# Merge and output projection of a hybrid encoder block: three chain steps per block of products in place of two

## The chip, the core and the metric

One core of one Trainium2 chip runs the whole layer in one launch. The metric is the device time of a run in microseconds (us). Before the change three runs took 2575.63, 2579.93 and 2582.38 us, median 2579.93 us.

## What is computed

The reference is one encoder layer on x, 2048 tokens of width 1024, all in float32. Cut to what matters here:

```python
h = rmsnorm(x, norm1_g); proj = h @ w_in
ya = windowed_gqa(...)            # 8 heads, band of +-128
ym = mlstm_branch(...)            # forward and backward recurrence, 4 heads of 128
gates = sigmoid(mg + merge_b)
u = gates[..., :1024] * (ya @ w_branch_attn) + gates[..., 1024:] * (ym @ w_branch_mlstm)
x = x + u @ w_out
# hier_moe on rmsnorm(x): group logits, expert logits, top 2 of 8 experts of the top group,
# tokens sorted by expert, silu(x @ w_gate) * (x @ w_up) @ w_down, added back by weight
```

The backward recurrence (`flip` in the reference) goes through the tokens from the last to the first. A merge of a token needs `ym` of both directions, and the routing of a token needs its merged x.

## The kernel before, in words

**Stages.** The program has three stages. F takes four chunks of 512 tokens (c = 0 to 3), makes all projections, the attention and the forward recurrence. B (merge and output projection) goes through the chunks backwards, c = 3, 2, 1, 0. M is the mixture of experts, one expert after the other. The change lies in B.

**Products of B.** A chunk has a BR part and a WO part. BR: four pieces of branch weights (`branch_piece`, 256 output columns each), and per piece two column blocks `cb`; a column block is 12 products of `yahi`/`yalo` (attention) and 12 of `ymhi`/`ymlo` (recurrence), 512 wide; so 192 products. `uevac` (L1157 to L1166) then merges the two sums by the gates on VectorE and splits the result into `uhi` (ScalarE, L1165) and `ulo` (VectorE, L1166). WO: four pieces of `w_out`, and per piece four groups `wo_group`, one for each 128 tokens, of 24 products 256 wide; so 16 groups, 384 products. `wevac` (L1173, VectorE) adds each group's sum to the residual tile `x1`. The sums of attention products and of WO groups lie in the PSUM pool `mmp`, two buffers.

**Weights.** `Stream.advance` brings a piece from memory on SP's queue (`wraw`, L220), splits it into a high half on ScalarE (`whi`, L236) and a low half on GpSimd (`wlo`, L239).

**Chains.** Everything else of B is written as generators in named queues of the class `Chains`: `mh` and `ml` (backward recurrence, `mhead` and `mtile`, four tiles of 128 tokens per chunk, one chunk ahead of the merge), `mp` (`mpost`: norm and gate of a tile's output, transposed at L812), `yp` (`yprep`: loads the next chunk's y tiles), and `rt` (`norm2` and `route` of the chunk merged before). `run_mms` writes the products and after each block of them (6 in BR, 12 in WO) lets the weight stream advance by one step and the chains by `tick_n[0]` steps, in turn over the queues:

```python
            if i % nsub == nsub - 1:
                if i == nsub - 1:
                    flush_late()
                ws.advance()
                ch.tick(tick_n[0])
```

`tick_n[0]` is 4 from the end of F until B's loop starts, 2 in B's loop, and 4 again for the last ten WO groups of c = 0. Where the chains are not done in time, `ch.drain` runs them to the end at once: `yp` at the start of BR, `ml` and `mp` ahead of the third WO piece. The order of writing is a priority: when the kernel is built, a scheduler puts each engine's instructions into their final order from it, and moves ready work ahead.

**How y reaches the merge.** `mpost` of a tile that is written after `direct["c"] = c - 1` was set (at a chunk's first WO piece) splits its transposed output straight from PSUM into `ymhi` (L817, ScalarE) and `ymlo` (L818, VectorE). A tile that is written earlier copies it to `hf` (L821, ScalarE) and stores it to `ym_s` in memory (L822, SP's queue); `yprep` loads it back into `yr` (L1136, SP's queue, two buffers) and splits it (L1138 on ScalarE, L1140 on VectorE).

**Routing.** `route` of a chunk computes the slots of its tokens: two counting products (L1298, L1299), then on VectorE the sum of the two choices (L1296 ahead of them), the slot numbers cast to integers (`si`, L1321) and the entries `ent`, one buffer: token numbers copied from the constant `tokid` (L1318) and weights (L1319). `put` (L1331) then writes them with eight indirect DMAs from GpSimd's queue into `slot_s`, each after the one before has landed. The token copies L1318 depend on nothing but `tokid` and the free buffer.

Of the kernel before, what the change touches and what calls it, by code (L numbers as in the profile page):

```python
# [102 lines left out]
def body(tc, A, out, scr_ext=None, upto="all"):  # L103
    nc = tc.nc
    scr_ext = scr_ext or {}
    es = ExitStack()
    with es:
        pass
        _body(tc, nc, A, out, scr_ext, upto, es)


def _body(tc, nc, A, out, scr_ext, upto, es):
# [213 lines left out]
    tick_n = [2]  # L326
# [1087 lines left out]
        held.extend((si, ent, i, 1) for i in range(2))  # L1414
        yield

    tick_n[0] = 2
    first_b = True
    while pi < len(plan):
        c, kind, i = plan[pi]  # L1420
# [440 lines left out]
```

## Time and profile before

| what | value |
|---|---|
| runs | 2575.63, 2579.93, 2582.38 us; median 2579.93 us |
| profiled execution | 2579.44 us, of which 2577.6 us are its span from the first to the last instruction |
| TensorE (PE) | 2420.9 us busy, 94% of the span |
| weight loads (PEld) | 2090.1 us, 81% |
| VectorE (DVE) | 1660.2 us, 64% |
| ScalarE (ACT) | 1312.2 us, 51% |
| GpSimd (POOL) | 931.0 us, 36% |
| mean granted TensorE clock | 0.977 of full speed |

Products are pipelined on TensorE and their ends are modelled, so a busy share near 100% still has slack in it; idle time in front of a product is idle. An engine's idle time before an instruction is given with what ended it. The stage that the change touches runs from about 1193 us to 1712 us of the span.

### The profile page before, as it was taken

Reading aid. Unit: us, or ns where it says so; the run is one execution under the profiler, and the core shown is the slowest. Engines: PE = TensorE matmul, PEld = TensorE weight load, DVE = VectorE, ACT = ScalarE, POOL = GpSimd, SP = SyncE. Lnnn points to the kernel's source line nnn. Section 1 sums busy time; section 2 is a strip of 40 time slices with the busy share of each in tenths; the row PEclk is TensorE's granted clock in tenths of the full one; section 3 lists DMA queues with packets and bytes.
Section 4 is the critical chain, followed back from the end, with each engine's and each line's share of the span. In section 5 each row is a group of like instructions: output and inputs, shape, how many; then the busy total and the mean of one; then the engine's idle time right before and its main releaser. Section 6 shows DMA issues by size and latency. Waiting matters only on the chain. (4 is left out here: it accounts for less than half of the span.)

```text
span 2577.6 us, 39210 instructions
## 1 busy us (share of the span) xinstructions
PE 2420.9 (94%) x13932; PEld 2090.1 (81%) x13933; DVE 1660.2 (64%) x2795; ACT 1312.2 (51%) x2564; POOL 931.0 (36%) x918
## 2 busy tenths in 40 slices
PE   7999999999999999997898889979999999999997
PEld 6889988899889989886787778867777777777776
DVE  4465455664556655578659484677866776778665
ACT  4455455464556555454342333236755665667554
POOL 5543444443543533333444445432221222122111
PEclk9999999999999999998999999989999999999999
DMA  4535434453445445556867565459998897889974
GB/s 146 162 116 169 148 109 125 144 181 94 127 138 158 134 121 163 182 174 193 244 193 209 176 180 168 131 192 322 363 318 294 255 328 235 299 255 361 343 245 103
DMA packets 348413, 515.33 MB, mean 200 GB/s; under 512 B 25019, under 2 KB 212500, under 8 KB 348188
## 3 DMA queue, kind: packets, MB, share of 16 engines
q1 hardware_dynamic: 332140, 460.03, 54.4%
q0 software_dynamic: 14880, 48.20, 8.0%
q10 hardware_dynamic: 1168, 4.21, 0.4%
q8 instruction: 127, 2.08, 0.3%
q14 instruction: 98, 0.80, 0.1%
HBM read 420.83 MB, written 91.54 MB: 199 GB/s over the span
## 5 line engine op out<-in xcount | busy, mean ns | idle before, releaser
L239 POOL TENSOR_TENSOR wlo<-wraw,whi 128x512 fp32r<-128x512 f32 (+1 forms) x422 | 574.1, 1390 | 403.2 <-ACT whi L236 386.4
L1573 DVE TENSOR_TENSOR elo<-raw,ehi 128x1024 fp32r<-128x1024 f32 x256 | 299.4, 1219 | 27.5 <-ACT ehi L1572 27.4
L319 PE MATMUL mm<-hThi,whi 128*128 128x512 f32 x768 | 306.4, 399 | 0.0
L319 PE MATMUL mm<-hTlo,whi 128*128 128x512 f32 x768 | 304.9, 397 | 0.0
L319 PE MATMUL mm<-hThi,wlo 128*128 128x512 f32 x768 | 303.6, 395 | 0.0
L236 ACT ACTIVATE whi<-wraw 128x512 fp32r<-128x512 f32 (+1 forms) x424 | 234.0, 622 | 130.0 <-PE mm L319 75.9
L319 PE MATMUL mm<-whi,hThi 128*128 128x256 f32 (+1 forms) x896 | 262.1, 292 | 3.0 <-ACT ev L908 1.8
L1572 ACT ACTIVATE ehi<-raw 128x1024 fp32r<-128x1024 f32 x256 | 254.1, 1050 | 19.7 <-DMA raw<-w_expert_up 17.8
L319 PE MATMUL mm<-wlo,hThi 128*128 128x256 f32 (+1 forms) x896 | 257.5, 287 | 1.5 <-POOL wlo L239 1.5
L319 PE MATMUL mm<-whi,hTlo 128*128 128x256 f32 (+1 forms) x896 | 258.1, 288 | 0.0
L1687 POOL DMA_INDIRECT out<-y,idx x32 | 55.4, 1731 | 448.8 <-DVE y L1686 223.2
L1619 PE MATMUL mm<-ehi,xhi 128*128 128x512 f32 x512 | 205.5, 401 | 0.0
L1619 PE MATMUL mm<-ehi,xlo 128*128 128x512 f32 x512 | 201.0, 393 | 0.4 <-DVE xlo L1598 0.4
L319 PEld LDWEIGHTS mm<-whi,hThi 128*128 128x128 f32 x896 | 172.3, 192 | 5.4 <-ACT ev L908 2.1
L319 PEld LDWEIGHTS mm<-wlo,hThi 128*128 128x128 f32 x896 | 172.4, 192 | 2.5 <-POOL wlo L239 1.8
L319 PEld LDWEIGHTS mm<-whi,hTlo 128*128 128x128 f32 x896 | 171.9, 192 | 0.9 <-DVE hTlo L449 0.2
L319 PEld LDWEIGHTS mm<-hThi,wlo 128*128 128x128 f32 x768 | 144.4, 188 | 31.1
L319 PEld LDWEIGHTS mm<-hThi,whi 128*128 128x128 f32 x768 | 144.6, 188 | 29.1
L319 PEld LDWEIGHTS mm<-hTlo,whi 128*128 128x128 f32 x768 | 144.5, 188 | 28.3
L1622 PE MATMUL mm<-elo,xhi 128*128 128x512 f32 x512 | 159.0, 392 | 0.0
L1573 DVE TENSOR_TENSOR elo<-rawd,ehi 128x1024 fp32r<-128x1024 f32 x128 | 151.4, 1220 | 11.6 <-ACT ehi L1572 11.4
L833 DVE SCALAR_TENSOR_TENSOR cacc<-cstg,colv,cacc 128x512 f32<-128x512 f32 x128 | 108.1, 845 | 58.4 <-ACT cacc L830 56.5
(456 smaller groups left out, 5932.0 us busy)
## 6 DMA issues: line engine op xcount, KB each, us to landing
wraw<-w_in SPq DMA_DIRECT2D x152, 512.0 KB, 4.3
raw<-w_expert_gate SPq DMA_DIRECT2D x128, 512.0 KB
raw<-w_expert_up SPq DMA_DIRECT2D x128, 512.0 KB, 10.1
rawd<-w_expert_down SPq DMA_DIRECT2D x64, 1024.0 KB, 12.5
mg_s<-evg SPq DMA_DIRECT2D x64, 256.0 KB, 3.8
gt<-mg_s SPq DMA_DIRECT2D x32, 512.0 KB, 6.5
wraw<-w_out SPq DMA_DIRECT2D x32, 512.0 KB, 7.3
mqk<-qk_s SPq DMA_DIRECT2D x16, 512.0 KB, 5.6
```

Of the source, the lines that this page charges most:

```text
L236: nc.scalar.activation(hi[:, ks, :W], r[:, k:k + 2, :W], AF.Copy)
L239: eng.tensor_sub(lo[:, ks, :W], r[:, k:k + 2, :W], hi[:, ks, :W].bitcast(F32))
L319: nc.tensor.matmul(o, l, r, start=st, stop=sp)
L833: nc.vector.scalar_tensor_tensor(acc, stg[:, r:r + CH], colv[:, j, r:r + 1], acc, op0=OP.mult, op1=OP.add)
L1572: nc.scalar.activation(dst[0], src, AF.Copy)
L1573: nc.vector.tensor_tensor(dst[1], src, dst[0].bitcast(F32), op=OP.subtract)
L1619: nc.tensor.matmul(self.gu[h], x_[:, k % 4, :], self.wt(k)[0][:, h, :], start=k == 0 and i == 0, stop=False)
L1622: nc.tensor.matmul(self.gu[h], self.xs[k // 4][0][:, k % 4, :], self.wt(k)[1][:, h, :], start=False, stop=k == KT - 1)
L1687: nc.gpsimd.indirect_dma_start(out=out, out_offset=bass.IndirectOffsetOnAxis(ap=self.idx, axis=0), in_=y, in_offset=None, compute_op=OP.add)
```

## The change

One number: the steps that the chains get after each block of products in B's loop, up to the last ten groups of c = 0.

```diff
@@ -1414,7 +1414,7 @@
         held.extend((si, ent, i, 1) for i in range(2))
         yield
 
-    tick_n[0] = 2
+    tick_n[0] = 3
     first_b = True
     while pi < len(plan):
         c, kind, i = plan[pi]
```

What it moves is seen in the built order alone. Up to the first merged column blocks of c = 3, and from the expert stage on, each engine's order is as it was; between them the number of TensorE rows is the same, and rows change places.

**TensorE, the counting products of the routing of c = 3's tokens.** First before, then with the change (`whi,uhi` are WO products, `yahi` and `ymhi` BR products, `mv`, `mw`, `Cst` the recurrence's, `mw` at L812 its output):

```order
L741 MATMUL m<-Cst,mqk 128x129
L1298 LDWEIGHTS before
L1298 MATMUL Rb<-ohb,before 128x4x32
L1299 LDWEIGHTS onesb
L1299 MATMUL Rb<-ohb,onesb 128x4x32
L319 MATMUL mm<-whi,ulo 128x256
```

```order
L1298 LDWEIGHTS before
L1298 MATMUL Rb<-ohb,before 128x4x32
L1299 LDWEIGHTS onesb
L1299 MATMUL Rb<-ohb,onesb 128x4x32
L741 MATMUL m<-Cst,mqk 128x129
L812 MATMUL m<-ident,mw 128x128 x4
L319 MATMUL mm<-yahi,wlo 128x512
```

They stood behind WO product 29 of c = 2 and stand now behind BR product 179 of it; for the routing of c = 2's tokens, behind WO product 5 of c = 1, now behind BR product 177. The outputs of the recurrence (L812) stood in c = 2 behind BR product 168 and WO products 76, 143 and 206, and stand behind BR product 179 and WO products 92, 191 and 222; in c = 1 the last stood behind WO product 196 and stands behind 224; in c = 3 the four stood behind BR products 96 and 169 and WO products 48 and 111, and stand behind BR products 66 and 133 and WO products 7 and 81.

**VectorE, the token copies in the WO part of c = 2.** Before, then with the change (`x_` are the residual tiles, one row per WO group; `hf`, `og`, `mw`, `Cst` are the recurrence's):

```order
L1173 SCALAR_TENSOR_TENSOR x_14384<-mm,x_14384 128x256
L1173 SCALAR_TENSOR_TENSOR x_14386<-mm,x_14386 128x256
L1318 COPY ent<-tokid 128x4 x2
L1173 SCALAR_TENSOR_TENSOR x_14380<-mm,x_14380 128x256
L1173 SCALAR_TENSOR_TENSOR x_14382<-mm,x_14382 128x256
```

```order
L772 SCALAR_TENSOR_TENSOR Cst<-Cst,mil,m 128x129 x2
L1173 SCALAR_TENSOR_TENSOR x_14515<-mm,x_14515 128x256
L808 TENSOR_TENSOR mw<-mw,og 128x512
L1318 COPY ent<-tokid 128x4 x2
L772 SCALAR_TENSOR_TENSOR Cst<-Cst,mil,m 128x129 x2
L1173 SCALAR_TENSOR_TENSOR x_14509<-mm,x_14509 128x256
```

The copies stood behind the 12th group of c = 2 and stand behind the 8th. The cast of the slot numbers (L1321) stood behind the 4th group and stands behind the 2nd. Between cast and copies lie 30 VectorE instructions before, 8 of them L1173, and 39 with the change, 6 of them L1173. In c = 1 the cast stands behind the 2nd group as before; the copies stood behind the 10th and stand behind the 7th, with 37 instructions between, 5 of them L1173.

**ScalarE, the recurrence's outputs in the WO part of c = 2.** Before, then with the change:

```order
L817 ACTIVATE ymhi<-m 128x4x128
L236 ACTIVATE whi<-wraw 128x2x256 x4
L748 ACTIVATE mdn<-m 128x2 x2
L817 ACTIVATE ymhi<-m 128x4x128
L236 ACTIVATE whi<-wraw 128x2x256 x4
L817 ACTIVATE ymhi<-m 128x4x128
```

```order
L821 ACTIVATE hf<-m 128x512
L236 ACTIVATE whi<-wraw 128x2x256 x4
L1138 ACTIVATE ymhi<-yr 128x4x128
L748 ACTIVATE mdn<-m 128x2 x2
L821 ACTIVATE hf<-m 128x512
L236 ACTIVATE whi<-wraw 128x2x256 x4
```

Before, seven of the twelve tiles went straight into `ymhi` (L817: one in c = 3, three in c = 2, three in c = 1). With the change none does: all twelve are copied (L821), stored and loaded back (L1138).

## Rows read from the trace of the kernel before

**Rows 1.** Busy time by engine, one stretch per part of B (BR, WO of c=3, 2, 1).

```profile
core 0: us, PE busy (x) PEld busy (x) DVE busy (x) ACT busy (x) POOL busy (x), PEclk, DMA share, GB/s
1192.80:1253.60 60.80, 54.58 (x252) 44.72 (x253) 50.71 (x82) 20.60 (x49) 27.98 (x34) 0.93 0.85 254
1253.70:1313.20 59.50, 55.29 (x452) 54.03 (x452) 24.36 (x48) 16.49 (x31) 24.01 (x21) 0.97 0.67 197
1313.20:1378.00 64.80, 62.03 (x333) 52.28 (x333) 54.67 (x102) 27.76 (x70) 29.53 (x29) 0.97 0.70 209
1378.00:1456.70 78.70, 61.52 (x481) 59.43 (x480) 44.16 (x97) 19.46 (x45) 35.02 (x36) 0.91 0.58 169
1456.70:1520.50 63.80, 61.41 (x340) 51.25 (x339) 55.36 (x107) 27.06 (x69) 31.24 (x30) 1.00 0.71 210
1520.50:1590.20 69.70, 58.41 (x472) 57.51 (x471) 38.80 (x86) 20.35 (x45) 35.50 (x33) 0.95 0.49 148
```

**Rows 2.** Timeline of VectorE, WO of c=2 (start us, us; idle before and releaser in brackets).

```profile
1405.07 1.24 DVE L1321 CAST si<-sl 128x8 int32<-128x8 f32 x1
...
1430.26 0.42 DVE L1173 SCALAR_TENSOR_TENSOR x<-mm,x 128x256 f32<-128x256 f32 x1 [2.42 <-PE mm L319]
1443.68 2.63 DVE L1318 COPY ent<-tokid 128x4 f32<-128x4 f32 x2 [12.99 <-DMA slot_s<-ent,si]
```

**Rows 3.** Timeline of TensorE, WO of c=2, around its longest idle time in B.

```profile
1435.75 0.38 PE L1201 MATMUL Tb<-ident,x 128*128 128x128 f32 x2
1446.70 0.69 PE L1201 MATMUL Tb<-ident,x 128*128 128x128 f32 x2 [10.57 <-DVE x L1173]
```

**Rows 4.** Timeline of weight loads right behind it, first and last of twelve.

```profile
1446.97 0.33 PEld L319 LDWEIGHTS mm<-whi,uhi 128*128 128x128 f32 x1
...
1449.32 0.33 PEld L319 LDWEIGHTS mm<-whi,ulo 128*128 128x128 f32 x1
```

**Rows 5.** Timeline of VectorE, WO of c=1.

```profile
1541.59 0.16 DVE L1321 CAST si<-sl 128x8 int32<-128x8 f32 x1
...
1569.01 0.43 DVE L1173 SCALAR_TENSOR_TENSOR x<-mm,x 128x256 f32<-128x256 f32 x1 [2.35 <-PE mm L319]
1575.48 0.24 DVE L1318 COPY ent<-tokid 128x4 f32<-128x4 f32 x2 [6.05 <-DMA slot_s<-ent,si]
```

**Rows 6.** Timeline of TensorE, WO of c=1; between the first two lie seven products.

```profile
1573.62 0.28 PE L319 MATMUL mm<-whi,uhi 128*128 128x256 f32 x1
...
1574.57 0.28 PE L319 MATMUL mm<-whi,ulo 128*128 128x256 f32 x1
1576.20 0.36 PE L319 MATMUL mm<-whi,uhi 128*128 128x256 f32 x1 [1.35 <-ACT whi L236]
```

**Rows 7.** Waits between engines over B, us in total, times, longest.

```profile
DVE ent L1318 <- DMA slot_s<-ent,si: 19.0, 2, 13.0
ACT ymhi L1138 <- DMA yr<-ym_s: 14.2, 5, 6.6
```

**Rows 8.** Groups of ScalarE instructions over B: busy, mean ns, idle before.

```profile
L817 ACT ACTIVATE ymhi<-m 128x512 fp32r<-128x512 f32 x7 | 4.1, 592 | 12.9 <-PE m L812 12.9
...
L1138 ACT ACTIVATE ymhi<-yr 128x512 fp32r<-128x512 f32 x5 | 3.2, 632 | 14.2 <-DMA yr<-ym_s 14.2
```

**Rows 9.** DMA issues over B: KB each, median us to landing.

```profile
yr<-ya_s SPq DMA_DIRECT2D x12, 256.0 KB, 3.6
```

**Rows 10.** Timeline of TensorE: idle times before L812, BR of c=3 and WO of c=1.

```profile
1245.05 1.09 PE L812 MATMUL m<-ident,mw 128*128 128x128 f32 x4 [4.56 <-DVE mw L757]
...
1554.92 0.63 PE L812 MATMUL m<-ident,mw 128*128 128x128 f32 x4 [3.22 <-DVE mdn L756]
```

**Rows 11.** One small VectorE instruction: all its durations (min/median/max ns), and its longest.

```profile
L755 DVE TENSOR_TENSOR mdn<-mdn,EN x64: 140/158/4071, 241.0 to 1554.2; 128x2 f32<-128x2 f32 x64
```

**Rows 12.** Timeline of GpSimd beside that longest one.

```profile
1550.28 3.74 POOL L239 TENSOR_TENSOR wlo<-wraw,whi 128x512 fp32r<-128x512 f32 x3
```

## The prediction

> **What bounds the kernel now.** I read the busy time by stretch first, then the waits between engines, then the timeline around TensorE's idle times, because the change only reorders and can only earn or cost idle time. In the table by part of B the reader is to compare a stretch's length with its TensorE time [rows 1]. TensorE is the bound nearly everywhere: in the BR parts of c = 2 and c = 1 it is busy 62.03 of 64.80 us and 61.41 of 63.80 us. It is idle 6.2 us in BR and 4.2 us in WO of c = 3, and 17.2 us (78.70 less 61.52) and 11.3 us (69.70 less 58.41) in the WO parts of c = 2 and c = 1. That is some 44 us with the 5.2 us of the two other BR parts, and no reordering can earn more than these. VectorE comes second: 50.71, 54.67 and 55.36 us in the BR parts, over four fifths of each, but only 24.36, 44.16 and 38.80 us in the WO parts [rows 1]. So a BR part has little room for more VectorE work and a WO part has much.
>
> The longest idle time of TensorE in B is 10.57 us in the WO part of c = 2 [rows 3]. Its cause is on VectorE: the token copies L1318, which belong to the next routing, stand in VectorE's queue 12.99 us until the eight writes of the routing before have let go of the one `ent` buffer [rows 2]. Behind them stand the L1173 that free the PSUM buffers, so TensorE runs dry. The same copies wait 6.05 us in c = 1 [rows 5], and only 1.35 us of that reach TensorE [rows 6]. These two are the whole 19.0 us of that wait [rows 7].
>
> **The change, part by part.** Nothing is added to the products. What moves is worth this.
>
> *The two stalls at the token copies.* Three times decide: how long the writes take from the cast L1321, how soon VectorE reaches the copies, and how long TensorE goes on meanwhile. From cast to release it is 1443.7 less 1406.3, 37.4 us, in c = 2 [rows 2] and 1575.5 less 1541.75, 33.7 us, in c = 1 [rows 5]. VectorE was there after 24.4 us (1430.7) and 27.7 us (1569.4). TensorE went on for 5.4 us, in c = 2 from 1430.7 to 1436.1 [rows 2, 3] and in c = 1 from 1569.4 to 1574.85 [rows 5, 6]: two groups, as many as `mmp` has buffers. Eight products take 0.95 us [rows 6], 0.119 us each, a group 2.86 us.
>
> With the change the copies come 6 groups behind the cast in c = 2 and 5 in c = 1, in place of 8 and 8. Six groups are 17.1 us, and some 36 products of the recurrence that now lie between, at about the same step of 0.11 us, 4 us more: 21 us. VectorE's own 39 instructions at 0.455 us (44.16 over 97, [rows 1]) are 17.8 us, so TensorE sets the pace. I add 3 us for waits of the recurrence inside and take 24 us, between 21 and 27. In c = 1 it is 14.3 and 3.5 us, with the same 3 us 21 us, between 18 and 25. For the writes I take 34 us in both, nearest to the 33.7 us, since in c = 2 one write more than usual came late; the ends are 33.7 and 37.4 us. TensorE then idles 34 less 24 less 5.4, 4.6 us, in c = 2 in place of 10.57: a gain of **6.0 us**. In c = 1 it idles 34 less 21 less 5.4, 7.6 us, in place of 1.35: a loss of **6.3 us**. The ends: c = 2 from 0.4 us worse (37.4, 21) to 9.3 better (33.7, 27); c = 1 from 12.7 worse (37.4, 18) to 2.0 worse (33.7, 25). Behind an idle time like the 10.57 us twelve weight loads take 0.33 us [rows 4]: TensorE is at the lower of its two levels (1.2 in place of 2.4 GHz) and starts a product every 0.21 us in place of 0.119, a cost of 1.1 us that now can come in both parts and is within these ends.
>
> *The earlier routing.* Its counting products go from WO into BR by some 40 to 50 products. Its VectorE work goes along, a few us, into BR parts where VectorE is busy over four fifths; a BR part is covered by TensorE, so I cost it at nothing. If that cover goes, `uhi` is late and TensorE waits at the first WO product.
>
> *The recurrence.* Only in c = 3 does it come earlier, by 30 to 41 products. In c = 2 and c = 1 its outputs come later by 11 to 48 products, because the routing takes the added steps and VectorE has no more to give there. In c = 3 about 2 us of recurrence products leave WO, and the idle time of 4.56 us before L812 in BR [rows 10] may shrink or move. WO of c = 3 has 4.2 us idle, BR 6.2 us. I take a gain of **2 us**, between 6 us gained (more than half of the 10.4) and 4 us lost (one more wait like 4.56).
>
> *Seven tiles by way of memory.* They lose L817 and L818 and get L821, a store and a load on SP's queue, L1138 and L1140. On TensorE nothing changes, ScalarE gets 0.63 us more for each [rows 8], 4.4 us in all, where it is busy a third of the time [rows 1]: hidden. The wait is not: the five tiles that went this way waited 14.2 us for their load, 2.8 us each [rows 7], with the splits of the next weights, L748 of the next tile and, over VectorE's L1140, the L1173 behind them in line. Seven more make 20 us of ScalarE waiting. A landing is 3.6 us [rows 9], so a store and a load take 7.2 us. That is two and a half groups, about what TensorE can run ahead. I take **1.5 us** on the path, between 0 and 10 (half of the 20). SP's queue carries seven stores and seven loads more, each load behind its store; what stands behind them there are loads for tiles and pieces ahead, which cost nothing while they have a group's time to spare.
>
> The Trainium skill, on the page DMA: Bandwidth & Descriptors, section Rules for kernel authors, says that a DMA that reads what an earlier one wrote must be held until the first one's completion, and puts the fixed cost of a DMA at about 2 us. By that fixed cost the way through memory would be an estimated 4 us and not 7.2 us, no wait would be left of the 2.8 us, and the sum would be 1.5 us lower. The row of 3.6 us speaks for the longer time.
>
> *Sum.* From 2579.44 us: less 6.0, plus 6.3, less 2, plus 1.5 gives 2579.2, so **2579 us**. The profiled execution lies 0.5 us under the median of the runs, 2579.93; I count against either alike. Differences within 0.3%, 7.7 us, cannot be told from no change here.
>
> **The rivals.**
>
> *Slower: the copies stop both WO parts.* The mechanism is the first term at its bad end: VectorE reaches the copies after 21 and 18 us, and the writes take 37.4 us. Then TensorE idles 11.0 us in c = 2 and 14.0 us in c = 1, 0.4 and 12.7 us more than now: 2592.5 us. It decides once the copies in c = 1 come under about 19 us behind the cast. For it: the copies stand 2 to 4 groups earlier, and cover is counted in groups. Against it: 7 to 9 more VectorE instructions lie between, and each wait of the recurrence there shortens the stall.
>
> *Slower: VectorE's small steps are caught by GpSimd.* One L755, usually 0.158 us, took 4.07 us [rows 11], from 1549.98 us on, while GpSimd made low halves of weights from 1550.28 to 1554.02 us [rows 12], and TensorE then idled 3.22 us before L812 [rows 10]. Of the eight outputs of c = 2 and c = 1 one was caught so. With all four outputs of each chunk closer to the writes, four caught would make 12.9 us in place of 3.2: 2589 us. Against it: as many steps and weight splits as before, only shifted. The Trainium skill, page SBUF — State Buffer, section Who interferes with whom, has this as a rule: a VectorE instruction and a GpSimd instruction that want the port they share exclude each other for a whole instruction. The caught L755 agrees with it, 4.07 us against 0.158.
>
> *Faster: the stalls go.* If the waits of the recurrence hold VectorE back until the writes have landed, in both parts, 10.57 and 1.35 us go, and with 4 us in c = 3 the time is 2563.5 us. For it: routing now starts up to two groups earlier in c = 2. Against it: in c = 1 the cast stands behind the same group as before, so there the copies only moved closer.
>
> *The change does not do what it says.* Three steps speed up the recurrence only where steps are what it lacks. In c = 2 and c = 1 it came later, so this is half true already; if terms one and four are small as well, the time is 2577 to 2581 us, inside the forecast.
>
> **How the numbers follow.** No telling difference, my forecast with the last rival: 0.48, its own range 2572 to 2587 us. The copies' stall 0.17 and the caught steps 0.10, together 0.27 slower. Faster 0.25. Low 2567 us leaves out about half of the faster case, high 2592 us about a third of the slower ones, together near 0.2.
>
> **What would show it.** In the changed profile: the wait of L1318 for `slot_s` nearer 5 to 13 us in both chunks than 13.0 and 6.1; TensorE's idle time in WO of c = 2 under 10.57 us and in c = 1 over 1.35 us; no L817; twelve L1138 from `ym_s`, with 25 to 40 us of waiting in place of 14.2; the parts of c = 0 and all outside B as long as before to 1 us or 2. The forecast is wrong if the two stalls move the same way, if ScalarE's waits show up as TensorE's idle time over 5 us, or if a BR part grows by over 5 us because VectorE has become its bound.

## The result, and the profile after

The change makes the kernel slower: 2594.25 us (median of 9 runs, 2588.54 to 2603.50) against 2578.48 us (median of 9 runs on the same chip), a ratio of 1.0057 with a 95% interval of 1.0043 to 1.0072. That is 14.7 us at the ratio itself, above the forecast's range (2567 to 2592 us). On another chip the same kernel gave 1.0057 again (1.0039 to 1.0074). The profiled execution took 2590.8 us, its span 2588.8 us.

First the same view as [rows 1] for the kernel after, with the two parts of c = 0 added (stretch, its length, then busy time and instructions of PE, PEld, DVE, ACT, POOL; the granted clock is the third number from the right):

```profile
1194.30:1251.36 57.06, 54.99 (x269) 45.89 (x270) 50.76 (x89) 20.74 (x51) 27.49 (x34) 0.97 0.92 272
1251.36:1310.23 58.87, 53.72 (x431) 52.96 (x430) 25.81 (x40) 17.70 (x31) 24.05 (x21) 0.94 0.68 204
1310.23:1376.58 66.35, 61.84 (x333) 51.83 (x332) 56.37 (x112) 28.11 (x71) 30.21 (x28) 0.97 0.71 205
1376.58:1457.96 81.38, 66.39 (x497) 64.55 (x496) 44.88 (x88) 20.53 (x44) 34.98 (x36) 0.87 0.66 184
1457.96:1520.37 62.41, 59.17 (x318) 49.04 (x317) 51.33 (x102) 27.11 (x68) 29.16 (x28) 1.00 0.71 213
1520.37:1600.60 80.23, 65.61 (x494) 63.33 (x493) 44.06 (x92) 21.51 (x47) 35.23 (x34) 0.89 0.53 153
1600.60:1651.84 51.24, 51.05 (x253) 42.04 (x251) 35.84 (x72) 19.28 (x36) 26.79 (x22) 1.00 0.74 216
1651.84:1723.49 71.65, 61.80 (x481) 60.27 (x479) 36.16 (x123) 16.85 (x34) 28.58 (x26) 0.90 0.28 84
```

Against [rows 1] c = 3 is 4.4 us shorter (115.9 in place of 120.3 us), BR of c = 2 and c = 1 differ by 1.5 us, WO of c = 2 is 2.7 us longer, and WO of c = 1 is 10.5 us longer. The WO part of c = 0 was 66.7 us before; it is 71.7 us now. The parts do not hold the same work, though: recurrence products moved from BR into WO. WO of c = 1 has 494 TensorE instructions in place of 472, which at the recurrence's step of 0.11 us is an estimated 2.4 of the 10.5 us; 3.3 us are idle time (14.6 in place of 11.3 us), and the rest is the same work taking longer.

The whole of B in one row tells more than the parts. These are B's first to last product in the kernel before, the kernel before profiled once more, the kernel after, and the kernel after once more:

```profile
1192.79:1709.10 516.31, 465.49 (x3062) 421.32 (x3062) 345.65 (x713) 167.49 (x374) 238.47 (x229) 0.96 0.62 184
```

```profile
1189.25:1703.53 514.28, 465.80 (x3061) 420.70 (x3062) 344.89 (x713) 166.88 (x374) 240.65 (x229) 0.96 0.61 185
```

```profile
1194.30:1723.49 529.19, 474.58 (x3062) 429.91 (x3062) 345.20 (x713) 171.84 (x381) 236.50 (x229) 0.94 0.64 186
```

```profile
1193.55:1726.33 532.78, 473.45 (x3062) 427.07 (x3062) 345.10 (x713) 170.89 (x381) 237.47 (x229) 0.95 0.63 185
```

TensorE does the same 3062 instructions in all four (the second row misses one record). It is busy 465.5 and 465.8 us before, 474.6 and 473.5 us after: 8.4 us more for the same work, on the mean. Its idle time (length less busy) is 50.8 and 48.5 us before, 54.6 and 59.3 us after: 7.3 us more. So **over half of the loss of 15.7 us is not idle time at all but TensorE at its lower clock level.** The second profile of the kernel before was taken to see whether that is chance; it is not. One sees it in single rows: behind the longest idle time of WO of c = 1 the weight loads of the kernel after take 0.33 us and products start 0.21 us apart, as in [rows 4].

```profile
1573.22 0.29 PEld L319 LDWEIGHTS mm<-whi,uhi 128*128 128x128 f32 x1 [7.21 <-DVE x L1173]
1573.38 0.34 PEld L319 LDWEIGHTS mm<-wlo,uhi 128*128 128x128 f32 x1
1573.60 0.33 PEld L319 LDWEIGHTS mm<-whi,ulo 128*128 128x128 f32 x1
```

Counted over B, 74 and 76 such loads of L319 last over 0.30 us before, 166 and 138 after. At 0.21 in place of 0.119 us each [rows 4, 6] the 77 more make an estimated 7 of the 8.4 us.

Now the idle times, by the waits between engines over B (us in total, times, longest), which answer to [rows 7]:

```profile
ACT ymhi L1138 <- DMA yr<-ym_s: 49.5, 11, 9.3
DVE h L1223 <- POOL rs L198: 34.6, 12, 6.6
DVE ymlo L1140 <- ACT ymhi L1138: 28.6, 11, 6.3
PE mm L319 <- DVE x L1173: 17.8, 7, 7.0
```

The wait of L1318 for `slot_s` is down from 19.0 us in two to 5.1 us in one, but the wait of `ymhi` L1138 is up from 14.2 to 49.5 us, and VectorE's wait behind it, at L1140, to 28.6 us (4.0 us before). The last row is what TensorE pays: it waits 17.8 us for an L1173 to free its PSUM buffer. The two rows of that wait in the kernel before make 12.3 us:

```profile
PE Tb L1201 <- DVE x L1173: 10.6, 1, 10.6
PE mm L319 <- DVE x L1173: 1.7, 1, 1.7
```

The long idle time of WO of c = 2 [rows 3] is gone, and two others stand in its place. In TensorE's timeline (the second is one of several rows around 1431 us):

```profile
1413.52 0.58 PE L319 MATMUL mm<-whi,uhi 128*128 128x256 f32 x1 [4.82 <-DVE x L1173]
...
1431.40 0.47 PE L812 MATMUL m<-ident,mw 128*128 128x128 f32 x1 [4.16 <-DVE mw L808]
```

The first comes by way of memory. On SP's queue the tile is stored and loaded back,

```profile
1399.88 0.39 SPq L822 DMA_DIRECT2D ym_s<-hf  x1
1404.21 0.32 SPq L787 DMA_DIRECT2D hf<-hf_s  x1
1404.58 0.43 SPq L1136 DMA_DIRECT2D yr<-ym_s  x1
```

then ScalarE splits it,

```profile
1409.09 0.63 ACT L1138 ACTIVATE ymhi<-yr 128x512 fp32r<-128x512 f32 x1 [9.35 <-DMA yr<-ym_s]
```

and VectorE, in order, stands at L1140 with the L1173 of a finished group behind it; the L1140 itself then takes 2.44 us in place of the usual 0.69. Further down, the copies L1318 come with no wait, right behind one very long L808:

```profile
1394.06 0.69 DVE L709 TENSOR_TENSOR mw<-mw,mib 128x512 f32<-128x512 f32 x1
...
1409.75 2.44 DVE L1140 TENSOR_TENSOR ymlo<-yr,ymhi 128x512 fp32r<-128x512 f32 x1 [6.29 <-ACT ymhi L1138]
...
1413.05 0.41 DVE L1173 SCALAR_TENSOR_TENSOR x<-mm,x 128x256 f32<-128x256 f32 x1
...
1425.62 5.72 DVE L808 TENSOR_TENSOR mw<-mw,og 128x512 f32<-128x512 f32 x1
1431.26 0.23 DVE L1318 COPY ent<-tokid 128x4 f32<-128x4 f32 x2
```

The cast L1321 of that routing began at 1393.98 us, just ahead of the first row; so the copies come 37 us behind it, after all eight writes. Without the long L808 VectorE would have been there some 5 us sooner.

In c = 1 the copies do wait, and TensorE is idle 7.01 us behind them where it was idle 1.35 us [rows 5, 6]. VectorE, then TensorE:

```profile
1536.09 0.16 DVE L1321 CAST si<-sl 128x8 int32<-128x8 f32 x1
...
1570.72 2.12 DVE L1318 COPY ent<-tokid 128x4 f32<-128x4 f32 x2 [5.10 <-DMA slot_s<-ent,si]
1572.75 0.41 DVE L1173 SCALAR_TENSOR_TENSOR x<-mm,x 128x256 f32<-128x256 f32 x1
```

```profile
1565.93 0.28 PE L319 MATMUL mm<-whi,ulo 128*128 128x256 f32 x1
1573.22 0.58 PE L319 MATMUL mm<-whi,uhi 128*128 128x256 f32 x1 [7.01 <-DVE x L1173]
```

### The profile page after: what moved, and what is told of

It is laid out like the page before. It is cut to its first block, busy times and chain, and to the rows that moved or that the text cites. A ratio compares the mean times of both kernels' runs of the same rounds, so it can differ in the third digit from the quotient of the medians.

```text
span 2588.8 us, 39263 instructions
## 1 busy us (share of the span) xinstructions
PE 2429.9 (94%) x13932; PEld 2099.2 (81%) x13933; DVE 1659.9 (64%) x2795; ACT 1315.5 (51%) x2571; POOL 929.5 (36%) x918
## 5 line engine op out<-in xcount | busy, mean ns | idle before, releaser
L319 PE MATMUL mm<-hThi,whi 128*128 128x512 f32 x768 | 306.4, 399 | 0.0
L319 PE MATMUL mm<-hTlo,whi 128*128 128x512 f32 x768 | 304.9, 397 | 0.0
L319 PE MATMUL mm<-hThi,wlo 128*128 128x512 f32 x768 | 303.6, 395 | 0.0
L236 ACT ACTIVATE whi<-wraw 128x512 fp32r<-128x512 f32 (+1 forms) x424 | 234.1, 622 | 90.5 <-PE mm L319 50.5
L319 PE MATMUL mm<-whi,hThi 128*128 128x256 f32 (+1 forms) x896 | 261.4, 292 | 3.0 <-ACT ev L908 1.8
L319 PE MATMUL mm<-wlo,hThi 128*128 128x256 f32 (+1 forms) x896 | 257.1, 287 | 1.1 <-POOL wlo L239 1.1
L319 PE MATMUL mm<-whi,hTlo 128*128 128x256 f32 (+1 forms) x896 | 257.9, 288 | 0.0
L319 PEld LDWEIGHTS mm<-whi,hThi 128*128 128x128 f32 x896 | 171.9, 192 | 5.4 <-ACT ev L908 2.1
L319 PEld LDWEIGHTS mm<-wlo,hThi 128*128 128x128 f32 x896 | 171.8, 192 | 2.1 <-POOL wlo L239 1.4
L319 PEld LDWEIGHTS mm<-whi,hTlo 128*128 128x128 f32 x896 | 171.5, 191 | 0.8 <-DVE hTlo L449 0.2
L319 PEld LDWEIGHTS mm<-hThi,wlo 128*128 128x128 f32 x768 | 144.3, 188 | 31.1
L319 PEld LDWEIGHTS mm<-hThi,whi 128*128 128x128 f32 x768 | 144.6, 188 | 29.1
L319 PEld LDWEIGHTS mm<-hTlo,whi 128*128 128x128 f32 x768 | 144.5, 188 | 28.3
L319 PE MATMUL mm<-whi,uhi 128*128 128x256 f32 x448 | 135.7, 303 | 27.1 <-DVE x L1173 17.8
L1573 DVE TENSOR_TENSOR elo<-rawd,ehi 128x1024 fp32r<-128x1024 f32 x128 | 151.4, 1219 | 14.1 <-ACT ehi L1572 14.0
## 6 DMA issues: line engine op xcount, KB each, us to landing
raw<-w_expert_up SPq DMA_DIRECT2D x128, 512.0 KB, 10.5
```

The source lines that it names most:

```text
L236: nc.scalar.activation(hi[:, ks, :W], r[:, k:k + 2, :W], AF.Copy)
L319: nc.tensor.matmul(o, l, r, start=st, stop=sp)
L1573: nc.vector.tensor_tensor(dst[1], src, dst[0].bitcast(F32), op=OP.subtract)
```

## The experiments

From this came three theories. **A, the way through memory**: twelve tiles in place of five stop ScalarE at L1138 and VectorE at L1140. **B, the token copies**: L1318 comes too early behind the cast. **C, the denser steps** themselves, whatever waits. All runs are against the kernel before on the same chip. The table gives, for each, the ratio with its interval, and from its one profile the length of B with TensorE's busy and idle time in it, and the length of WO of c = 1 (us). A profiled execution lies up to 7 us from the median of its kernel (e21: 2584.14 against 2591.39 us), and two profiles of one kernel differ by 2 and 3.6 us in B, so smaller differences in the last four columns prove little.

| kernel | ratio | B | busy | idle | WO, c = 1 |
|---|---|---|---|---|---|
| before (two profiles) | 1 | 516.3, 514.3 | 465.5, 465.8 | 50.8, 48.5 | 69.7, 69.2 |
| after (two profiles) | 1.0057 (1.0043 to 1.0072) | 529.2, 532.8 | 474.6, 473.5 | 54.6, 59.3 | 80.2, 78.4 |
| e1 after, tiles held | 1.0060 (1.0045 to 1.0075) | 524.7 | 475.4 | 49.3 | 76.4 |
| e2 before, all by memory | 1.0114 (1.0097 to 1.0130) | 537.9 | 476.1 | 61.8 | 73.4 |
| e9 before, three `ent` | 0.9992 (0.9980 to 1.0004) | 511.2 | 474.5 | 36.7 | 67.0 |
| e10 after, three `ent` | 1.0054 (1.0038 to 1.0069) | 527.7 | 473.1 | 54.6 | 76.6 |
| e5 three steps in c = 3 | 1.0007 (0.9996 to 1.0017) | 517.5 | 471.4 | 46.1 | 70.7 |
| e13 three steps in WO | 1.0020 (1.0011 to 1.0030) | 523.9 | 471.9 | 52.0 | 77.9 |
| e12 three steps in BR | 1.0086 (1.0069 to 1.0103) | 535.7 | 476.6 | 59.1 | 74.8 |
| e20 no round trip | 1.0088 (1.0074 to 1.0101) | 526.9 | 474.3 | 52.6 | 76.5 |
| e28 no round trip, three `ent` | 1.0066 (1.0044 to 1.0089) | 522.6 | 470.1 | 52.5 | 69.1 |
| e11 tiles held, three `ent` | 1.0045 (1.0030 to 1.0060) | 524.7 | 471.3 | 53.4 | 76.0 |
| e19 later split | 1.0001 (0.9990 to 1.0011) | 514.2 | 471.9 | 42.3 | 69.7 |
| e21 later split, c = 1's loads | 1.0060 (1.0043 to 1.0078) | 523.4 | 474.6 | 48.8 | 77.9 |
| e22 later split, c = 0's loads | 1.0047 (1.0029 to 1.0064) | 521.5 | 469.5 | 52.0 | 77.2 |
| e23 later split, three `ent` | 0.9983 (0.9968 to 0.9998) | 510.8 | 471.4 | 39.4 | 68.6 |

Two rows with two `ent` buffers (e3, e4) are told below.

### Theory A: does the way through memory make the loss?

First the change with the seven tiles held ahead of L812 until they may go directly:

```diff
-                next(q[0])
-                return True
+                held = next(q[0]) == "hold"
+                return not held
...
+        while direct.get("c") != t // TPC and t % TPC in ((0, 1, 2), (0, 1, 2), (0,), ())[t // TPC]: yield "hold"
         p = mps.tile([P, 4, P], F32, name="m")
```

> Three steps as in the change, but the seven tiles that went directly into ymhi and ymlo before the change are held ahead of their transpose L812 until their chunk may be written, so that they go directly again (seven L817, five L1138 of ymhi). Theory A, the way through memory: the loss of 15 us is ScalarE standing at L1138 for a load, VectorE at L1140 behind it, and TensorE dry; without it the time falls to 2576 to 2584 us, and the wait of ymhi L1138 from 49.5 to under 20 us. Theory B, the token copies: L1318 comes as early as with the change, so the time stays at 2590 to 2597 us. Theory C, the denser steps themselves: also 2590 to 2597 us.

The wait at L1138 fell to what it was before the change, and the time did not move: 1.0060. The row of its waits over B:

```profile
ACT ymhi L1138 <- DMA yr<-ym_s: 13.5, 5, 5.7
```

But the held outputs came late and close together (behind WO products 142, 192 and 224 in c = 1), so this run alone decides nothing against A. Its mirror is the kernel before with the permission taken away:

```diff
         if kind == "wo" and i == 0:
-            direct["c"] = c - 1
+            pass
```

> Two steps as before, but the permission to write directly is never given after c = 3, so that the same twelve tiles go through memory as with the change. Theory A (way through memory): 2588 to 2598 us, with over 40 us of waiting at ymhi L1138. Theories B (token copies) and C (denser steps): 2577 to 2584 us, since neither copies nor steps come closer.

At two steps the way is dear: 1.0114, with 62.9 us of waiting at L1138. Most of it lies in the BR parts of c = 2 and c = 1 (72.6 and 74.1 us in place of 64.8 and 63.8 us), where the kernel after loses next to nothing (66.4 and 62.4 us); so it lies in another place than the change's. (The routing was pushed back too: the counting products stand behind WO products 91, 86 and 19.)

Next the change with loads that need not wait for the store:

```diff
-                        src[:, :, t * P:(t + 1) * P].rearrange("j p q -> p j q")
+                        (src if c == NCH - 1 else ya_s)[:, :, t * P:(t + 1) * P].rearrange("j p q -> p j q")
```

> The change, but for the twelve tiles of c = 2 to 0 the load L1136 reads the attention's y, which lies in memory long since, in place of the recurrence's; the store L822 stays. So the kernel leaves out that the load waits for the store (its merge sees other numbers). ScalarE's L1138 and VectorE's L1140 stay. Theory A (way through memory): the wait of ymhi L1138 falls from 49.5 to under 20 us, B is 8 to 15 us shorter than with the change (529 us from its first to its last product), ratio 0.998 to 1.002. Theory C (denser steps, whatever way the tiles go): B stays within 4 us of 529 us, ratio 1.004 to 1.007.

The wait at L1138 halved (26.2 us), B stayed at 526.9 us, inside what theory C gave. The ratio, 1.0088, holds an expert stage that got other tokens: what follows B took 876.9 us in place of 868.5 and 865.4 us in the two profiles of the kernel before, 8 to 11 us; without them the ratio is 1.0043 to 1.0055. **The round trip is not the cause by itself.** In this run the copies L1318 wait again, 15.7 us in two.

### Theory B: do the copies make the loss?

Two `ent` buffers, on the change and on the kernel before:

```diff
-        ent = bp.tile([P, 2, n, 2], F32, name="ent")
+        ent = bp.tile([P, 2, n, 2], F32, name="ent", bufs=2)
```

> The change with two ent buffers in place of one, so that the token copies L1318 wait for no slot write. Theory B (token copies): the loss goes, 2576 to 2584 us. Theory A (way through memory): only the 5.1 us wait of L1318 in c = 1 with its 7.0 us of idle TensorE can go, 2586 to 2594 us. Theory C: 2590 to 2597 us.

> The kernel before with two ent buffers. If the two stalls at the token copies are worth what the trace shows (10.57 and 1.35 us of idle TensorE, and about 1 us of half clock): 2566 to 2571 us. If another wait takes their place: 2576 to 2581 us. It measures the term of the two stalls by itself.

The change with two gave 1.0049 (1.0034 to 1.0064), the kernel before with two 0.9999 (0.9985 to 1.0012). The second taught how not to do it. VectorE's timeline there:

```profile
1437.96 2.39 DVE L1318 COPY ent<-tokid 128x4 f32<-128x4 f32 x2 [12.01 <-DMA slot_s<-ent,si]
```

The second routing's copies had become free and had moved far ahead; the third's, which need the first buffer back, took their place at the same spot and waited 12.01 us. Three buffers, `bufs=3`, leave nothing to wait for:

> The kernel before with three ent buffers, one for each of the three routings of four tiles. With two the builder's scheduler had put the third routing's copies L1318 at the same place in c = 2, and they still waited 12.0 us there; with three no copy can wait for a slot write. If the stalls are worth what the trace shows: no wait of L1318 for slot_s, TensorE's idle time before L1201 in WO of c = 2 gone, and a ratio to the kernel before of 0.995 to 0.997 (8 to 12 us less). If another wait takes their place: 0.999 to 1.001.

> The change with three ent buffers. Theory B (token copies make the loss): the ratio to the kernel before is 0.998 to 1.001. Theories A (way through memory) and C (denser steps): two buffers already left one wait of 5 us less and gave 1.0049, so 1.003 to 1.006, with 45 to 52 us of waiting at ymhi L1138.

Both without any wait of L1318. In the kernel before TensorE's idle time falls by 12 to 14 us, to 36.7 us, and its busy time rises by 9 us, to 474.5 us: the ratio is 0.9992, no telling gain. On the change it is 1.0054, nothing gained either. In place of the 7.01 us behind the copies there is now, a little later, an idle time of 4.75 us (VectorE, then TensorE; L807 and L808 take 0.69 us as a rule):

```profile
1571.23 1.76 DVE L807 TENSOR_TENSOR mw<-mw,mrs 128x512 f32<-128x512 f32 x1 [2.53 <-POOL mrs L198]
1573.02 1.64 DVE L808 TENSOR_TENSOR mw<-mw,og 128x512 f32<-128x512 f32 x1
1574.58 0.41 DVE L1173 SCALAR_TENSOR_TENSOR x<-mm,x 128x256 f32<-128x256 f32 x1
```

```profile
1574.80 0.45 PE L812 MATMUL m<-ident,mw 128*128 128x128 f32 x1 [4.75 <-DVE mw L808]
```

A late output of the recurrence stops TensorE where the copies did. **Theory B falls as the whole cause**: the copies' wait is real, but without it the next wait is due.

### Where do three steps cost?

Three runs with three steps in some parts only; the first is shown, the others have `kind == "wo"` and `kind == "br"` as the condition:

```diff
     while pi < len(plan):
-        c, kind, i = plan[pi]
+        c, kind, i = plan[pi]; tick_n[0] = 3 if c == NCH - 1 else 2
```

> Three steps in c = 3 alone, two from c = 2 on (six tiles direct, six through memory). By the lengths of the parts with the change (c = 3 4.5 us shorter, c = 2 4.2 longer, c = 1 9.0 and c = 0 3.9 longer): if each chunk's loss hangs on its own steps, c = 3 gains 3 to 5 us and the rest is as before, ratio 0.998 to 0.9995. If c = 3's earlier recurrence pushes c = 2's routing and copies as it does in the order (counting products behind BR product 179 of c = 2), c = 2 loses its 4 us too: 0.9995 to 1.001. If the loss comes from c = 3 on: 1.003 or more.

In c = 3 alone three steps cost and earn nothing, 1.0007; the loss is not carried in from c = 3. This is the middle case of what was expected, but its 4 us in WO of c = 2 are not seen (78.9 us).

> Three steps after the blocks of the WO parts, two in the BR parts. Seven tiles go directly, as before the change, with no tile held; the outputs of the recurrence in c = 2 and c = 1 and the routing of c = 1 stand where the change has them. Theory A (way through memory): ratio 0.998 to 1.002. Theory C (denser steps: more of the chains' work in the WO parts of c = 2 and c = 1): WO of c = 1 is 5 to 11 us longer than before, ratio 1.003 to 1.006. Theory B (copies): the copies' stall in c = 1 is 5 us or more, ratio 1.002 to 1.005.

In WO alone they cost 1.0020, with WO of c = 1 as long as after the change, 77.9 us, though seven tiles go directly. No theory fits both: the ratio is at the edge of A and of B, the part is as C had it, and the copies' wait there is 3.9 us.

> Three steps after the blocks of the BR parts, two in the WO parts: the twin of three in WO alone (1.002, seven tiles direct). All twelve tiles go through memory. Theory A (way through memory): most of the loss comes with the twelve tiles, ratio 1.004 to 1.011. Theory C (denser steps in the WO parts): 0.998 to 1.002, since the steps in WO are as before. If the two halves simply add up to the change's 1.0057: 1.003 to 1.005.

In BR alone, 1.0086, inside the range of theory A: but the two halves add up to nearly twice the change, so they are not parts of one sum. In BR alone the order looks like that of e2 (all twelve tiles through memory, counting products late: WO products 32, 32 and 19), and so does the time.

### The later split

The most telling edit leaves the twelve tiles on their way through memory and only writes two more steps between load and split:

```diff
             nc.sync.dma_start(r, src)
-            yield
+            for _ in range(3): yield
             nc.scalar.activation(hi, r, AF.Copy)
```

> The change with two more chain steps between a tile's load L1136 and its split L1138, so that the load has longer to land; on TensorE the outputs of the recurrence in c = 2 and c = 1 come earlier by it (behind WO products 48, 140, 187 and 42, 120, 211). Theory A (way through memory): what counts is how long ScalarE stands at L1138; if that falls under 25 us the ratio is 0.999 to 1.003, if it stays over 40 us, 1.004 to 1.007. Theory C (denser steps): 1.004 to 1.007 in either case.

> The kernel before once more, for a second profile. In the first one B's 516.3 us hold 50.0 us of TensorE's idle times over 0.3 us and 12.1 us lost to products at the lower clock level; with the change 53.8 and 19.7 us. If the 7.6 us of lower clock are the change's, the second profile shows 11 to 14 us again; if they are chance, it can show 17 to 20 us with the idle time as before.

The later split takes the whole loss away, 1.0001. And the wait that I took for the cause is all there (waits over B):

```profile
ACT ymhi L1138 <- DMA yr<-ym_s: 52.8, 12, 9.8
DVE ymlo L1140 <- ACT ymhi L1138: 30.3, 11, 6.7
PE mm L319 <- DVE x L1173: 10.3, 5, 4.0
```

52.8 us at L1138 and 30.3 us at L1140 are as much as after the change (49.5 and 28.6); what fell is TensorE's wait for L1173, from 17.8 to 10.3 us. **With this, theory A falls as the whole cause, and C too**: three steps and twelve tiles through memory run as fast as the kernel before. TensorE's busy time stays 6.3 us above that of the kernel before, and its idle time is 7.3 us below. What differs is the built order. The outputs L812 stand in c = 1 behind WO products 42, 120 and 211 in place of 92, 192 and 224, in c = 2 behind 48, 140 and 187 in place of 92, 191 and 222. The second profile of the kernel before is read above.

Is it one chunk's order? The later split for the loads of c = 1 only, then of c = 0 only:

```diff
-            yield
+            for _ in range(3 if c == 1 else 1): yield
```

> The change with the two more steps between load and split for the loads of c = 1 alone (they run in WO of c = 2). The outputs of the recurrence in c = 2 stand as with the change (WO products 92, 191, 222); those of c = 1 stand early again (BR product 174, WO products 72, 147, 198 in place of WO 1, 92, 192, 224); c = 0 starts as with the change. Theory E (the loss comes with outputs of the recurrence that were moved late into a WO part, chunk by chunk): c = 1's 9 us go, ratio 1.001 to 1.0035. Theory A (way through memory): twelve tiles as before, over 45 us of waiting at ymhi L1138, ratio 1.004 to 1.007.

> The change with the two more steps for the loads of c = 0 alone (they run in WO of c = 1). The outputs of the recurrence stand as with the change in c = 2 and c = 1, and only the order of c = 0 is that of before (counting products of c = 1's tokens behind BR product 188 in place of 164). Theory E: c = 2 and c = 1 keep their loss, c = 0 gives back its 4 us, ratio 1.003 to 1.005. If the wait at L1138 in c = 1 is what counts: 1.000 to 1.003.

With the outputs of c = 1 early again, WO of c = 1 is still 77.9 us and the ratio 1.0060, as theory A had it: theory E falls in its simple form. The waits in WO of c = 1, where no copy L1318 waits:

```profile
DVE ymlo L1140 <- ACT ymhi L1138: 12.6, 3, 8.7
PE mm L319 <- DVE x L1173: 10.2, 3, 4.3
```

But the three waits of TensorE come from three places: 3.96 us behind a wait of VectorE for `og` from memory (L805), 1.89 us behind an L1140 that itself took 5.06 us, and 4.33 us behind the wait of 8.7 us at L1140.

With c = 0's order put back the ratio is 1.0047, which fits c = 0's own share (its WO part is 68.4 us in place of 71.7) but cannot be told from 1.0057.

### Do the suspects stand in for one another?

What most slow profiles have in WO of c = 1 is a VectorE held ahead of an L1173; which wait holds it changes. (In e3 and e10 TensorE waits for a late output there, 5.3 and 4.75 us, and for an L1173 0.5 us at most.) So theory G: each of three suspects (way, copies, late outputs) can do it alone. Two runs test it, both put together from edits above.

> The kernel in which the loads do not wait for the store (they read the attention's y; its merge sees other numbers, and its expert stage was 11.6 us longer for it, 0.45%), now with three ent buffers as well. In it the outputs of the recurrence in c = 1 stand early (BR product 156, WO products 48, 129, 198), no load waits for a store and no copy for a slot write. Theory G (three suspects, each of which alone is enough to stop VectorE ahead of an L1173 in WO of c = 1): with all three gone that part is 67 to 72 us (76.5 us with one ent buffer), and the ratio falls from 1.0088 to 1.004 to 1.0065. If another cause makes the loss: the part stays at 75 to 79 us and the ratio at 1.007 to 1.010.

> The change with the seven tiles held so that they go directly, and three ent buffers: no way through memory beyond that of the kernel before, no wait at the token copies, but the outputs of the recurrence late (WO products 168, 192, 221 in c = 2; BR 177, WO 142, 192, 224 in c = 1). Theory G: the late outputs alone are enough, WO of c = 1 is 74 to 78 us and the ratio 1.003 to 1.006. If way and copies together are the loss: 68 to 72 us and 0.998 to 1.002.

The row of WO of c = 1 in e20 (copies waiting), in e28 (nothing left) and in e11 (late outputs alone):

```profile
1528.77:1605.25 76.48, 63.92 (x478) 62.90 (x476) 36.78 (x76) 20.67 (x45) 33.73 (x31) 0.89 0.49 147
```

```profile
1524.55:1593.61 69.06, 60.67 (x477) 59.85 (x476) 34.65 (x74) 20.21 (x44) 32.74 (x31) 0.93 0.55 162
```

```profile
1521.67:1597.66 75.99, 64.04 (x489) 62.37 (x488) 44.70 (x78) 18.92 (x42) 36.00 (x34) 0.91 0.46 137
```

69.1 us with all three gone and 76.0 us with late outputs alone, both as theory G had them; the ratio of e28, 1.0066, is a hair above its bound, with 4 to 7 us of it behind B (872.0 us) and WO of c = 2 still at 81.4 us, where its outputs stand late (behind 96, 185 and 231). In c = 1 G is shown for the copies: e20 and e28 have the same order of outputs and 478 and 477 TensorE instructions in that part, and differ by 7.4 us. For the late outputs e11 supports it; of its 6.9 us over e28 an estimated 1.3 are 12 more instructions. For the way through memory it is not shown: in e21 only part of the stop stands behind it, and e19 has it too, with 10.0 us of VectorE's waiting at L1140, in a part of 69.7 us. The longest wait there, 5.72 us, reached TensorE as 1.34 us, and the 8.7 us in e21 as 4.33; the rest of the 8.2 us between the two is 22 more instructions (2.4 us by estimate), other waits and the lower clock level. In c = 2 one profile says less: in e22, whose order there is the change's, WO took 76.8 us in place of 81.4 and 81.2 us (the long L808 was missing, see the last section).

### A version that beats both

> Three steps, the later split in all chunks and three ent buffers: the two edits that took idle time away, together, on the changed kernel. If they add up: 0.996 to 0.999, the fastest here. If what is taken off the idle time comes back at the lower clock level, as in the kernel before with three buffers: 0.999 to 1.001.

> The change once more, for a second profile and its ratio on this chip: 1.0043 to 1.0072. If the lower clock level is the change's and not chance: 18 to 21 us of B lost to it again, and 12 to 14 us more for B than the 514 to 516 us of the kernel before; if chance, 12 to 17 us.

Later split and three `ent` buffers on the changed kernel give 0.9983 (0.9968 to 0.9998), 4.4 us under the kernel before and the lowest here, though the interval only just leaves out no difference and overlaps that of e9 (0.9980 to 1.0004). The second run of the change repeats its ratio and its busy time; B is 16 to 18 us longer than in the kernel before, more than the 12 to 14 us expected. The row of e23:

```profile
1191.90:1702.71 510.81, 471.44 (x3064) 424.81 (x3062) 340.85 (x709) 170.75 (x381) 236.02 (x229) 0.95 0.65 193
```

Idle time is 9 to 11 us under that of the kernel before, busy time 6 us over it: what the edits earn comes back by over half at the lower clock.

## Why the prediction was wrong

- **The lower clock level.** The first step that failed is the premise that the change "can only earn or cost idle time". The same work took 8.4 us more of TensorE's busy time over B, the largest single term. I took the clock from one stretch, 1.1 us "within these ends", and gave it no term of its own. Why the level was lower for longer stays open.
- **The two stalls at the token copies.** The second step that failed is "TensorE sets the pace", with 3 us for waits inside. VectorE's own work between cast and copies was near the forecast 17.8 us (17.4 in c = 2 up to the long L808, 18.1 in c = 1), but it stood idle 14.1 and 11.2 us, where the forecast leaves some 6 and 4. So in c = 1 it came to the copies 29.4 us behind the cast and not 21. The writes took 34.5 us, as forecast, so the copies waited 5.1 us and not 13. That TensorE's idle time was still 7.01 and 7.58 us, near the forecast 7.6, is luck: TensorE went on for 0.6 us and not 5.4, because the last L1173 stood 3 us back, and the copies took 2.1 us in place of 0.24 [rows 5]. (The 1.35 us that I set against it stand in [rows 6] as ended by the weight split L236, so it is not sure that they were the copies' either.) In c = 2 VectorE was held by L1140 and then by one long L808, so the copies did not wait at all, as the rival of the stalls that go has it; but L1140 (4.82 us) and the output behind L808 (4.16 us) stopped TensorE in their place. The forecast gain of 6.0 us became 2.2 us less idle time (17.2 to 15.0 us) in the first pair of profiles and 0.5 us more (15.2 to 15.7 us) in the second. I priced one stall at a time, as if nothing were due behind it. The kernel before without any such wait (e9) shows it plainly, 0.9992.
- **Seven tiles by way of memory.** 1.5 us was a guess between 0 and 10, with nothing on where the waits fall. The forecast waits (25 to 40 us at L1138) were 49.5 us. As the whole cause it is refuted (e19, e20); one stop of 4.82 us in c = 2 stands behind it, and in e21 one of 4.33. Its landing times: below.
- **The earlier routing.** Costed at nothing. BR kept its length as forecast, but WO of c = 0 went from 66.7 and 69.1 to 71.7 and 70.9 us, 3.4 us on the mean; "c = 0 as before to 1 us or 2" was wrong. With c = 0's order alone put back (e22) it was 68.4 us.
- **The recurrence.** The 2 us gained in c = 3 came as idle time: 10.4 and 10.0 us before, 7.2 and 7.8 after. In length c = 3 is 4.4 us shorter in the first pair of profiles and 0.7 us longer in the second (118.3 against 117.6 us). Its outputs in c = 1 came later by up to 60 products (behind WO product 192 in place of 132), not 48.
- **The rivals.** The one with the copies gave 2592.5 us, close to the time, by a mechanism that falls: without any wait at the copies the loss is the same (1.0054). The caught steps are not the loss: between 1187 and 1740 us 36 and 33 VectorE instructions took over 1 us more than the median of their line before, 36 and 33 after, and all that VectorE took above its medians is 67.7 and 68.1 us before, 65.3 and 64.0 after. They only fell in other places.

The marks of "wrong" that I had set were met by ScalarE's waits: 4.82 us in one place, 5.4 us with 0.55 us behind the next such wait.

## What to carry to other kernels

Where two or three waits stand close behind one another on an engine that frees TensorE's buffers, removing one brings out the next, and the loss of a new order is not the sum of its waits: test by taking them away together, too. Price an idle time of TensorE with the clock that follows it, by the busy time of the same instructions in two profiles, not by the idle time alone, and count a part's instructions before comparing its length. More steps for background chains are only worth what the built order makes of them; look first at where a load's consumer stands; here writing it further behind its load took the loss away.

## What was not expected of the hardware

- **The clock.** What an idle time costs behind it is not fixed. An idle time of 3.22 us before L812 in WO of c = 1 of the kernel before [rows 10] was followed by no long weight load; in its second profile 3.25 us at the same place were followed by eleven. And the edit that took 12 to 14 us of idle time away (e9) left TensorE at the lower level for longer (busy 474.5 in place of 465.5 us, granted clock over B 0.95 in place of 0.96), not shorter.
- **One large VectorE instruction caught for 5.72 us, or not.** All durations of L808 (min, median, max in ns) in the kernel after, and in e22, whose order up to there is the same:

```profile
L808 DVE TENSOR_TENSOR mw<-mw,og x16: 678/684/5723, 1112.8 to 1574.6; 128x512 f32<-128x512 f32 x16
```

```profile
L808 DVE TENSOR_TENSOR mw<-mw,og x16: 677/684/1030, 1109.8 to 1571.8; 128x512 f32<-128x512 f32 x16
```

In the kernel after, the L808 that began at 1425.62 us lasted as long as GpSimd made four low halves in a row:

```profile
1425.85 4.93 POOL L239 TENSOR_TENSOR wlo<-wraw,whi 128x512 fp32r<-128x512 f32 x4
```

In e22 the same L808 began at 1426.47 us, 0.94 us ahead of GpSimd's four, and took 0.68 us. In the second profile of the change it was caught again (5.73 us). The copies behind it in e22 then wait after all, and TensorE is idle 1.70 us there in place of 4.16:

```profile
1430.33 2.15 DVE L1318 COPY ent<-tokid 128x4 f32<-128x4 f32 x2 [3.19 <-DMA slot_s<-ent,si]
```

So up to 2.5 us of TensorE's idle time hang on less than a microsecond between two engines. The Trainium skill, page SBUF — State Buffer, section Who interferes with whom, says that VectorE and GpSimd exclude each other at the port they share for a whole instruction; the 5.72 us fit that, but here the hold lasted through four GpSimd instructions, and L808 had begun 0.23 us ahead of the first.
- **A store and a load back of 256 KB.** From the issue of the store (1399.88 us) SP issued nothing until 1404.21 us; the load went out at 1404.58 us and ScalarE could start at 1409.09 us: 9.2 us in all. I had put it at 7.2 us. The Trainium skill, page DMA: Bandwidth & Descriptors, section Anatomy of one DMA — SWDGE (gpsimd) path, puts a DMA issued from GpSimd at about 2 us and its bytes at 436 GB/s. That would be 2.6 us for 256 KB and an estimate of 5.2 us for two; these were issued from SP, and the trace decides for the longer time.
